# Row sums of |x - y|: the absolute values of the last row go to PSUM instead of SBUF

## The chip, the cores and the metric

The kernel runs on one core of a Trainium2 chip. The metric is the device time of an execution in microseconds (us), lower is better. Of every kernel some executions are timed and one is profiled. A run counts as slow when it is over 1.5% above the fastest of the same kernel, and as unknown when it is a single one; all the timed runs compared here were of the fast state, and the granted clock in their records was 1.0. Ratios are computed as the mean time of one kernel's fast runs over the mean of the other's in the same rounds, so they aren't quite the ratios of the medians that are quoted. "The span" is the time from the first to the last instruction of the profiled run; it is some 1.6 us shorter than the device time (82.8 beside 84.4 us).

Engines: VectorE (DVE in the profile) subtracts, ScalarE (ACT) takes absolute values and sums, the sync engine (SPq) issues transfers (DMA) from HBM, where x and y lie. ACTIVATE is the name of ScalarE's instruction in the profile. TensorE has no work. SBUF and PSUM are the memories in which the kernels allocate their tensors; the kernel before keeps its rows and sums in SBUF alone.

## The reference

```python
x, y = randn(1024, 4096), randn(1024, 4096)      # float32
np.sum(np.abs(x - y), axis=-1)                    # 1024 sums, float32
```

## The kernel before

Each of the 128 partitions holds 8 rows of 4096 columns. Rows 0 to 3 of x and y are loaded whole; the later y rows go into the buffers of the earlier ones, each after the subtraction that frees it. Rows 5 and 6 are worked in halves, and the last row in five pieces of 1728, 1024, 640, 384 and 320 columns, so that little work is left after the last byte has come (1.04 us, from 80.27 to 81.31 us of the span).

```python
def sub(tx, ty, waits):                       # VectorE: tx = tx - ty, in place
    for s, v in waits:
        put(lambda: nc.vector.wait_ge(s, v))
    put(lambda: nc.vector.tensor_sub(out=tx, in0=tx, in1=ty).then_inc(s_sub, 1))
    count[0] += 1

def absum(tx, to, sem):                       # ScalarE: |tx| in place, its sum into one column
    put(lambda: nc.scalar.wait_ge(s_sub, count[0]))
    put(lambda: nc.scalar.activation(tx, tx, ABS, accum_out=to).then_inc(sem, 1))
    count[1] += sem is s_act
# ... rows 0 to 6 ...
for i, w in enumerate(PIECES):                # the last row
    c = slice(o, o + w)
    tx, ty = xb[:, H - 1, c], yb[:, H - 1, c]
    # ... (i == 2: a small reduce of the sums of rows 5 and 6) ...
    if i < n_part:                            # the first four pieces
        sub(tx, ty, [(s_piece[i], 32)])
        absum(tx, last[:, i:i + 1], s_end)
    else:                                     # the last piece: VectorE alone
        put(lambda: nc.vector.wait_ge(s_piece[i], 32))
        put(lambda: nc.vector.tensor_sub(out=last[:, n_part:n_part + w], in0=tx, in1=ty).then_inc(s_end, 1))
        put(lambda: nc.vector.wait_ge(s_end, n_part + 2))
        put(lambda: nc.vector.reduce_sum(out=ro[:, K - 1:K], in_=last, axis=AX, apply_absolute_value=True).then_inc(s_end, 1))
    o += w
put(lambda: nc.sync.wait_ge(s_end, n_part + 3))
put(lambda: nc.sync.dma_start(out=orr, in_=ro).then_inc(s_out, 16))
```

The closing reduce runs over ScalarE's four sums and the last piece's 320 differences together, and so it needs two engines: VectorE's last subtraction and ScalarE's last sum. In the trace a second instruction, ACTIVATION_READ_ACCUMULATOR (below: the accumulator read) of 185 to 188 ns, follows each of the 13 ACTIVATEs; the semaphore update that VectorE waits for is recorded on it, and comes 8 ns after its end.

Of the kernel before, what the change touches and what calls it, by code (L numbers as in the profile page):

```python
# [6 lines left out]
F32 = mybir.dt.float32  # L7
ABS = mybir.ActivationFunctionType.Abs
AX = mybir.AxisListType.X

F32 = mybir.dt.float32
ABS = mybir.ActivationFunctionType.Abs
# [6 lines left out]
class Entry:  # L19
# [5 lines left out]
    def put(self, emit, before="UnconditionalBranch"):  # L25
        nc = self.nc
        hook = nc.inst_callbacks[-1]
        lower = nc._always_lower_symbolic_ap
        nc.remove_inst_callback(hook)
        nc._always_lower_symbolic_ap = False  # L30
        here = nc.cur_bb.bb.instructions
        n = len(here)
        try:
            emit()
        finally:
            nc._always_lower_symbolic_ap = lower
            nc.push_inst_callback(hook)
        here = nc.cur_bb.bb.instructions
        main = nc.main_func.blocks[0].instructions
        while len(here) > n:  # L40
            mine = here.pop(n)
            first = next(i for i, x in enumerate(main) if x.engine == mine.engine and x.opcode == before)
            main.insert(first, mine)
# [22 lines left out]
@with_exitstack  # L66
def kernel(ctx, tc, x, y, axis, out):
    nc = tc.nc
    P = nc.NUM_PARTITIONS
    R, C = x.shape  # L70
    K = R // P
    xr = x.rearrange("(p k) c -> p k c", p=P, k=K)
    yr = y.rearrange("(p k) c -> p k c", p=P, k=K)
    orr = out.rearrange("(p k) -> p k", p=P, k=K)
    assert sum(PIECES) == C and sum(HALVES) == C
    n_part = len(PIECES) - 1
    n2 = len(HALVES)
    H = K // 2
    entry = Entry(nc)
    put = entry.put  # L80


    def sbuf(name, shape):
        return nc.alloc_sbuf_tensor(name, shape, F32, align_bytes=256).ap()

    xa = sbuf("xa_rows", [P, H, C])
    xb = sbuf("xb_rows", [P, H, C])

    yb = sbuf("yb_rows", [P, H, C])
    ro = sbuf("ro_sums", [P, K])  # L90
    half = sbuf("half_sums", [P, 2, n2])

    last = sbuf("last_piece", [P, n_part + PIECES[-1]])

    s_first = tc.alloc_semaphore("s_first")
    s_xb = tc.alloc_semaphore("s_xb")
    s_row = [tc.alloc_semaphore(f"s_row{k}") for k in range(H - 1)]
    s_piece = [tc.alloc_semaphore(f"s_piece{i}") for i in range(len(PIECES))]
    s_sub = tc.alloc_semaphore("s_sub")
    s_act = tc.alloc_semaphore("s_act")  # L100
    s_end = tc.alloc_semaphore("s_end")

    s_out = nc.alloc_semaphore("s_out")


    for r in (slice(0, 1), slice(1, H)):
        put(lambda: nc.sync.dma_start(out=xa[:, r, :], in_=xr[:, r, :]).then_inc(s_first, 16), before="Drain")
    put(lambda: nc.scalar.dma_start(out=yb, in_=yr[:, 0:H, :]).then_inc(s_first, 16))
    put(lambda: nc.sync.dma_start(out=xb[:, 0:H - 1, :], in_=xr[:, H:K - 1, :]).then_inc(s_xb, 16))
    for k in range(H - 1):  # L110
        put(lambda: nc.sync.wait_ge(s_sub, k + 1))
        put(lambda: nc.sync.dma_start(out=yb[:, k, :], in_=yr[:, H + k, :]).then_inc(s_row[k], 16))
    o = 0
    for i, w in enumerate(PIECES):
        c = slice(o, o + w)
        put(lambda: nc.sync.dma_start(out=xb[:, H - 1, c], in_=xr[:, K - 1, c]).then_inc(s_piece[i], 16))  # L116
        if i == 0:
            put(lambda: nc.sync.wait_ge(s_sub, H))
        put(lambda: nc.sync.dma_start(out=yb[:, H - 1, c], in_=yr[:, K - 1, c]).then_inc(s_piece[i], 16))  # L119
        o += w  # L120


    count = [0, 0]

    def sub(tx, ty, waits):
        for s, v in waits:
            put(lambda: nc.vector.wait_ge(s, v))
        put(lambda: nc.vector.tensor_sub(out=tx, in0=tx, in1=ty).then_inc(s_sub, 1))  # L128
        count[0] += 1

    def absum(tx, to, sem):
        put(lambda: nc.scalar.wait_ge(s_sub, count[0]))
        put(lambda: nc.scalar.activation(tx, tx, ABS, accum_out=to).then_inc(sem, 1))  # L133
        count[1] += sem is s_act

    for k in range(H):
        sub(xa[:, k, :], yb[:, k, :], [(s_first, 48)] if k == 0 else [])
        absum(xa[:, k, :], ro[:, k:k + 1], s_act)
    sub(xb[:, 0, :], yb[:, 0, :], [(s_xb, 16), (s_row[0], 16)])
    absum(xb[:, 0, :], ro[:, H:H + 1], s_act)  # L140

    for k in (1, 2):
        o = 0
        for i, w in enumerate(HALVES):
            c = slice(o, o + w)
            sub(xb[:, k, c], yb[:, k, c], [(s_row[k], 16)] if i == 0 else [])
            absum(xb[:, k, c], half[:, k - 1, i:i + 1], s_act)
            o += w
    done56 = count[1]
    o = 0  # L150
    for i, w in enumerate(PIECES):
        c = slice(o, o + w)
        tx, ty = xb[:, H - 1, c], yb[:, H - 1, c]
        if i == 2:
            put(lambda: nc.vector.wait_ge(s_act, done56))
            put(lambda: nc.vector.reduce_sum(out=ro[:, K - 3:K - 1], in_=half, axis=AX).then_inc(s_end, 1))  # L156
        if i < n_part:
            sub(tx, ty, [(s_piece[i], 32)])
            absum(tx, last[:, i:i + 1], s_end)
        else:  # L160
            put(lambda: nc.vector.wait_ge(s_piece[i], 32))
            put(lambda: nc.vector.tensor_sub(out=last[:, n_part:n_part + w], in0=tx, in1=ty).then_inc(s_end, 1))  # L162
# [6 lines that stand above are left out]
    entry.at_end(lambda: nc.sync.wait_ge(s_out, 16).then_inc(s_out, -16))  # L169
# [35 lines left out]
```

## Time and profile before

| What | Before |
|---|---|
| Median of the first three runs | 84.38 us (84.36 to 84.47) |
| Span of the profiled run | 82.8 us |
| VectorE, ScalarE busy | 36.4 us (44%), 31.5 us (38%) |
| Read from HBM | 33.55 MB, 405 GB/s over the span |
| ACTIVATEs of the last row (1728, 1024, 640, 384) | 1627, 1040, 726, 513 ns |
| Accumulator read | 186 ns |
| Last subtraction (320), closing reduce | 492, 491 ns |

Neither compute engine is busy half of the time: they wait for data (VectorE for the first of y until 41.1 us), and DMA's busy share is 94 to 100% in the stretches from 20 to 76.6 us. The chain of waits and the timeline of the end are shown in the prediction. There, each row's start and duration are in us, and an entry in brackets tells how long the engine was idle before it and for whom.

### The profile page before, as it was taken

Reading aid. Unit: us, or ns where it says so; the run is one execution under the profiler, and the core shown is the slowest. Engines: PE = TensorE matmul, PEld = TensorE weight load, DVE = VectorE, ACT = ScalarE, POOL = GpSimd, SP = SyncE. Lnnn points to the kernel's source line nnn. Section 1 sums busy time; section 2 is a strip of 40 time slices with the busy share of each in tenths; the row PEclk is TensorE's granted clock in tenths of the full one; section 3 lists DMA queues with packets and bytes.
Section 4 is the critical chain, followed back from the end, with each engine's and each line's share of the span. In section 5 each row is a group of like instructions: output and inputs, shape, how many; then the busy total and the mean of one; then the engine's idle time right before and its main releaser. Section 6 shows DMA issues by size and latency. Waiting matters only on the chain.

```text
span 82.8 us, 104 instructions
## 1 busy us (share of the span) xinstructions
DVE 36.4 (44%) x16; ACT 31.5 (38%) x27; POOL 0.2 (0%) x4
## 2 busy tenths in 40 slices
DVE  0000000000000000000199999999279898999772
ACT  2400000000000000000000988979690599999990
POOL 0000000000000000000000000000000000000000
DMA  5992999989999999998888999859999999999950
GB/s 127 404 807 103 538 538 435 451 388 451 435 451 435 419 467 419 404 451 380 380 380 380 451 617 451 380 253 404 475 388 467 419 404 406 427 413 412 401 195 2
DMA packets 2592, 33.56 MB, mean 405 GB/s; under 512 B 416, under 2 KB 928, under 8 KB 1696
## 3 DMA queue, kind: packets, MB, share of 16 engines
q1 hardware_dynamic: 2448, 25.17, 72.3%
q10 hardware_dynamic: 144, 8.39, 23.4%
HBM read 33.55 MB, written 0.00 MB: 405 GB/s over the span
## 4 chain that ended last, share of the span: by engine, by line
DMA 63%; DVE 22%; SPq 10%; issue 1%
DMA yb_rows<-in_y_dram 63%; DVE xa_rows L128 21%; SPq L116 6%; SPq L119 4%; DVE last_piece L162 1%; DVE ro_sums L164 1%
## 5 line engine op out<-in xcount | busy, mean ns | idle before, releaser
L128 DVE TENSOR_TENSOR xa_rows<-xa_rows,yb_rows 128x4096 f32<-128x4096 f32 x4 | 17.4, 4420 | 41.1 <-DMA yb_rows<-in_y_dram 41.1
L133 ACT ACTIVATE xa_rows<-xa_rows 128x4096 f32<-128x4096 f32 x4 | 14.5, 3617 | 44.5 <-DVE xa_rows L128 44.5
L128 DVE TENSOR_TENSOR xb_rows<-xb_rows,yb_rows 128x2048 f32<-128x2048 f32 (+5 forms) x9 | 17.9, 2015 | 3.5 <-DMA yb_rows<-in_y_dram 3.5
L133 ACT ACTIVATE xb_rows<-xb_rows 128x2048 f32<-128x2048 f32 (+5 forms) x9 | 15.1, 1681 | 3.0 <-DVE xb_rows L128 2.9
L133 ACT ACT_TABLE_LOAD x1 | 1.3, 1283 | 1.7 <-PEq L186 1.7
L133 ACT ACTIVATION_READ_ACCUMULATOR xb_rows<-xb_rows 128x1 f32 x9 | 1.7, 186 | 0.0
L133 ACT ACTIVATION_READ_ACCUMULATOR xa_rows<-xa_rows 128x1 f32 x4 | 0.7, 186 | 0.0
L162 DVE TENSOR_TENSOR last_piece<-xb_rows,yb_rows 128x320 f32<-128x320 f32 x1 | 0.5, 492 | 0.3 <-DMA yb_rows<-in_y_dram 0.3
L164 DVE TENSOR_REDUCE ro_sums<-last_piece 128x1 f32<-128x324 f32 x1 | 0.5, 491 | 0.0
L156 DVE TENSOR_REDUCE ro_sums<-half_sums 128x2 f32<-128x4 f32 x1 | 0.1, 150 | 0.0
L186 POOL MEMSET const-bfloat16-1.0<- 128x1 bf16 x1 | 0.1, 101 | 0.0
L186 POOL MEMSET const-uint8-127<- 128x1 uint8 x1 | 0.1, 101 | 0.0
L186 POOL MEMSET const-float32-0.0<- 128x1 f32 x1 | 0.1, 98 | 0.2 <-issue 0.2
L186 POOL MEMSET const-float32-1.0<- 128x1 f32 x1 | 0.1, 98 | 0.0
## 6 DMA issues: line engine op xcount, KB each, us to landing
xa_rows<-in_x_dram SPq DMA_DIRECT2D x1, 6144.0 KB, 36.9
xb_rows<-in_x_dram SPq DMA_DIRECT2D x1, 6144.0 KB, 54.4
yb_rows<-in_y_dram SPq DMA_DIRECT2D x3, 2048.0 KB, 15.4
xa_rows<-in_x_dram SPq DMA_DIRECT2D x1, 2048.0 KB, 17.0
xb_rows<-in_x_dram SPq DMA_DIRECT2D x1, 864.0 KB, 17.7
yb_rows<-in_y_dram SPq DMA_DIRECT2D x1, 864.0 KB, 15.8
xb_rows<-in_x_dram SPq DMA_DIRECT2D x1, 512.0 KB, 16.6
yb_rows<-in_y_dram SPq DMA_DIRECT2D x1, 512.0 KB, 17.4
```

Of the source, the lines that this page charges most:

```text
L116: put(lambda: nc.sync.dma_start(out=xb[:, H - 1, c], in_=xr[:, K - 1, c]).then_inc(s_piece[i], 16))
L119: put(lambda: nc.sync.dma_start(out=yb[:, H - 1, c], in_=yr[:, K - 1, c]).then_inc(s_piece[i], 16))
L128: put(lambda: nc.vector.tensor_sub(out=tx, in0=tx, in1=ty).then_inc(s_sub, 1))
L133: put(lambda: nc.scalar.activation(tx, tx, ABS, accum_out=to).then_inc(sem, 1))
L156: put(lambda: nc.vector.reduce_sum(out=ro[:, K - 3:K - 1], in_=half, axis=AX).then_inc(s_end, 1))
L162: put(lambda: nc.vector.tensor_sub(out=last[:, n_part:n_part + w], in0=tx, in1=ty).then_inc(s_end, 1))
L164: put(lambda: nc.vector.reduce_sum(out=ro[:, K - 1:K], in_=last, axis=AX, apply_absolute_value=True).then_inc(s_end, 1))
L186: nc = _bacc.Bacc("TRN2", target_bir_lowering=False, num_devices=1)
```

## The change

ScalarE's in-place output of the last row's first four pieces is written to a PSUM tensor instead. Nobody reads these values. The intent is a shorter ACTIVATE near the end of the kernel.

```diff
+    absd = nc.alloc_psum_tensor("abs_piece", [P, C], F32).ap()
...
-    def absum(tx, to, sem):
+    def absum(tx, to, sem, out=None):
         put(lambda: nc.scalar.wait_ge(s_sub, count[0]))
-        put(lambda: nc.scalar.activation(tx, tx, ABS, accum_out=to).then_inc(sem, 1))
+        put(lambda: nc.scalar.activation(tx if out is None else out, tx, ABS, accum_out=to).then_inc(sem, 1))
...
-            absum(tx, last[:, i:i + 1], s_end)
+            absum(tx, last[:, i:i + 1], s_end, absd[:, c])
```

## The prediction

The sum came to 84.38 + 0.00 = 84.38 us. The savings were its terms for ScalarE: the earlier ones were held to become idle time, the last one to lie beside the last subtraction, so that they counted as 0.00 in it.

> **What bounds the kernel now.** I read four views: the chain that ended last, to see which work sets the end; the list of groups with the shapes kept apart, for the durations of the instructions concerned; the waits, for who was kept idle; and the timeline of the last six microseconds, where the change takes place. The chain on the page:
>
> ```profile
> ## 4 chain that ended last, share of the span: by engine, by line
> DMA 63%; DVE 22%; SPq 10%; issue 1%
> DMA yb_rows<-in_y_dram 63%; DVE xa_rows L128 21%; SPq L116 6%; SPq L119 4%; DVE last_piece L162 1%; DVE ro_sums L164 1%
> ```
>
> ScalarE (ACT) isn't in it at all. The kernel reads 33.55 MB and the page's DMA rate is a mean of 405 GB/s; from 20 us to 76.6 us the stretches that I summed run at 408 to 427 GB/s with DMA busy for 94 to 100%. VectorE (DVE, 44% busy) and ScalarE (38%) follow the transfers. The timeline of the end (columns: start, duration, engine, line, operation, out<-in, shapes, and in brackets how long the engine sat idle before and for whom):
>
> ```profile
> 76.67 1.63 ACT L133 ACTIVATE xb_rows<-xb_rows 128x1728 f32<-128x1728 f32 x1
> 76.88 1.23 DVE L128 TENSOR_TENSOR xb_rows<-xb_rows,yb_rows 128x1024 f32<-128x1024 f32 x1 [0.28 <-DMA yb_rows<-in_y_dram]
> ...
> 78.21 0.19 ACT L133 ACTIVATION_READ_ACCUMULATOR xb_rows<-xb_rows 128x1 f32 x1
> 78.30 1.04 ACT L133 ACTIVATE xb_rows<-xb_rows 128x1024 f32<-128x1024 f32 x1
> 78.47 0.82 DVE L128 TENSOR_TENSOR xb_rows<-xb_rows,yb_rows 128x640 f32<-128x640 f32 x1 [0.30 <-DMA yb_rows<-in_y_dram]
> 79.25 0.19 ACT L133 ACTIVATION_READ_ACCUMULATOR xb_rows<-xb_rows 128x1 f32 x1
> 79.34 0.73 ACT L133 ACTIVATE xb_rows<-xb_rows 128x640 f32<-128x640 f32 x1
> 79.46 0.56 DVE L128 TENSOR_TENSOR xb_rows<-xb_rows,yb_rows 128x384 f32<-128x384 f32 x1 [0.17 <-DMA yb_rows<-in_y_dram]
> 79.97 0.19 ACT L133 ACTIVATION_READ_ACCUMULATOR xb_rows<-xb_rows 128x1 f32 x1
> 80.06 0.51 ACT L133 ACTIVATE xb_rows<-xb_rows 128x384 f32<-128x384 f32 x1
> 80.29 0.49 DVE L162 TENSOR_TENSOR last_piece<-xb_rows,yb_rows 128x320 f32<-128x320 f32 x1 [0.28 <-DMA yb_rows<-in_y_dram]
> 80.48 0.19 ACT L133 ACTIVATION_READ_ACCUMULATOR xb_rows<-xb_rows 128x1 f32 x1
> 80.82 0.49 DVE L164 TENSOR_REDUCE ro_sums<-last_piece 128x1 f32<-128x324 f32 x1
> 81.34 0.35 SPq L168 DMA_DIRECT2D out_dram<-ro_sums  x1
> ```
>
> Two things are to be seen. First, each of VectorE's last four subtractions was kept waiting by a transfer of y (0.17 to 0.30 us), none by ScalarE. Second, the closing reduce at L164 needs both the last subtraction and ScalarE's last sum. The subtraction ends at 80.29 + 0.49 = 80.78, and the reduce starts 0.04 later. ScalarE's last accumulator read ends at 80.48 + 0.19 = 80.67. A hand-over from VectorE to ScalarE took about the same 0.04 (the 384 subtraction ends at 79.46 + 0.56 = 80.02, its ACTIVATE starts at 80.06), so ScalarE alone would have let the reduce start at about 80.71. ScalarE has 80.82 - 80.71 = 0.11 us of slack there. VectorE's own list of waits confirms that nothing of ScalarE's held it:
>
> ```profile
> DVE xb_rows L128 <- DMA yb_rows<-in_y_dram: 1.1, 4, 0.4
> DVE last_piece L162 <- DMA yb_rows<-in_y_dram: 0.3, 1, 0.3
> ```
>
> [...] the 384 ACTIVATE lasts 513 ns and the 4096 one 3617 ns, so (3617 - 513)/3712 = 0.836 ns an element, which leaves 513 - 384 x 0.836 = 192 ns fixed, and the accumulator read follows the 384 ACTIVATE's start by 0.42 us, that is 0.10 us more than its elements take. The trace of before has no PSUM access, so the other side is not shown. [...]
>
> **The change part by part.** The instruction lists of the two kernels have the same rows on every engine in the same order; only the main output of four ACTIVATEs (1728, 1024, 640 and 384 columns) is in another memory. Nothing is added: nobody reads the absolute values, only the sums, which still go to the same SBUF column. No semaphore count, DMA or wait changes. The nine other ACTIVATEs stay in place.
>
> [...] The 1728 ACTIVATE starts at 76.67 because of the one before it, which is unchanged. [...] the 640 subtraction ends at 78.47 + 0.82 = 79.29, so the start is 79.33 instead of 79.34. The 384 one likewise waits for its subtraction (80.02) and starts at 80.06, as before. So from the 640 piece on ScalarE is held by VectorE and the earlier savings become idle time. [...] On the path: 0.00 us. Even four ACTIVATEs that cost nothing would leave the reduce at 80.82.
>
> Against it on the path: no instruction, transfer or wait is longer. The sum is 84.38 + 0 = 84.38 us.
>
> **The rivals.** (1) ScalarE writes PSUM more slowly than SBUF[...]. Since ScalarE is just caught up at the 640 and 384 pieces, a cost of d for each of the four would add up: the end moves by about 4d - 0.11, as only 0.01 us of idle time stands in the way (79.33 against 79.34). So d = 0.1 us makes 84.38 + 0.29 = 84.67, within 2%. For 2% (1.69 us) d must be (1.69 + 0.11)/4 = 0.45 us, 88% on top of the 384 one's 513 ns. If PSUM halved the rate for an element, the 3776 columns would cost 3776 x 0.836 = 3.16 us more: 84.38 + 3.16 - 0.11 = 87.4 us. Nothing in the trace speaks for that[...]. I give it 1%.
>
> (2) Fewer SBUF writes speed up VectorE or the transfers. The trace speaks against it for VectorE: the first 128x4096 subtraction ran alone (ScalarE started at 45.60, after it) and the other three beside ScalarE's writes, and all four took 4418 to 4426 ns. The subtractions also wait for data, so only the last one's 0.49 us and the reduce's 0.49 us could count; a tenth of these would be 0.1 us: 84.28. For the transfers, only the last 3.7 us could gain; at a few per cent that is 0.1 us too.
>
> (3) ScalarE's earlier finish moves something that starts a transfer. It can't: the sync engine's only waits before the output are on VectorE's subtractions, and all loads of the last row are issued by 67.57 + 1.76 = 69.33 us, before the first changed ACTIVATE.
>
> **Range and chances.** The expected effect is zero, with at most some 0.1 us either way, so the range is mostly the spread between runs. The three runs of before span 84.36 to 84.47; another round or chip may shift the DMA's pace, which sets 63% of the chain, by some tenths of a per cent: 0.3% is 0.25 us. I take 84.2 to 84.6. Faster by 2% would need 1.7 us; the whole stretch from the last arrival (80.27) to the end of the reduce (81.31) is only 1.04 us, and no part of that is ScalarE's: 0.5%. Slower by 2% is rival 1: 1%. The rest, 98.5%, is within 2%.
>
> **What would show it.** In the profile after: the four ACTIVATEs write abs_piece with durations below 1627, 1040, 726 and 513 ns[...]; ScalarE shows a new idle time ahead of the 640 or 384 one, released by VectorE; VectorE's waits in the last row still name transfers alone; the reduce starts 0.04 us after the last subtraction ends; the chain has no ScalarE in it. The prediction is wrong if the reduce is released by ScalarE's last accumulator read (rival 1), if subtractions of equal shape last differently or the last y piece lands earlier in time against the same DMA start (rival 2), or if fast runs of the two kernels differ by over 0.3% in the same rounds.

## The result, and the profile after

The changed kernel took 84.39 us (median of 4 runs, 84.29 to 84.44), the kernel before in the same rounds 84.42 us (4 runs, 84.36 to 84.58): ratio 0.9993, 95% interval 0.9978 to 1.0008. The interval leaves no room for a gain of 0.25%.

The chain that ended last, on the page of the changed kernel (its lines are numbered two higher than before):

```profile
## 4 chain that ended last, share of the span: by engine, by line
DMA 63%; DVE 22%; SPq 11%; issue 1%
DMA yb_rows<-in_y_dram 63%; DVE xa_rows L130 21%; SPq L118 6%; SPq L121 4%; DVE last_piece L164 1%; DVE ro_sums L166 1%
```

It has the same members as before with nearly the same shares, and still no ScalarE. The timeline of the last six microseconds of the changed kernel:

```profile
76.60 1.59 ACT L135 ACTIVATE abs_piece<-xb_rows 128x1728 f32<-128x1728 f32 x1
...
78.13 0.19 ACT L135 ACTIVATION_READ_ACCUMULATOR abs_piece<-xb_rows 128x1 f32 x1
78.22 1.01 ACT L135 ACTIVATE abs_piece<-xb_rows 128x1024 f32<-128x1024 f32 x1
78.44 1.51 DVE L130 TENSOR_TENSOR xb_rows<-xb_rows,yb_rows 128x640 f32<-128x640 f32 x2 [0.34 <-DMA yb_rows<-in_y_dram]
79.17 0.19 ACT L135 ACTIVATION_READ_ACCUMULATOR abs_piece<-xb_rows 128x1 f32 x1
79.30 0.71 ACT L135 ACTIVATE abs_piece<-xb_rows 128x640 f32<-128x640 f32 x1
79.94 0.19 ACT L135 ACTIVATION_READ_ACCUMULATOR abs_piece<-xb_rows 128x1 f32 x1
80.04 0.47 ACT L135 ACTIVATE abs_piece<-xb_rows 128x384 f32<-128x384 f32 x1
80.26 0.49 DVE L164 TENSOR_TENSOR last_piece<-xb_rows,yb_rows 128x320 f32<-128x320 f32 x1 [0.32 <-DMA yb_rows<-in_y_dram]
80.45 0.19 ACT L135 ACTIVATION_READ_ACCUMULATOR abs_piece<-xb_rows 128x1 f32 x1
80.79 0.49 DVE L166 TENSOR_REDUCE ro_sums<-last_piece 128x1 f32<-128x324 f32 x1
```

(The row x2 holds the subtractions of 640 and 384 columns.) The last subtraction ends at 80.26 + 0.49 = 80.75 and the reduce starts 0.04 later, as before. ScalarE's last accumulator read ends at 80.45 + 0.19 = 80.64, again 0.11 us before the subtraction's end.

But the same rows hold a surprise. The ACTIVATEs are shorter: 1595, 1006, 707 and 473 ns in the list of groups, against 1627, 1040, 726 and 513. Yet the distance from an ACTIVATE's start to its accumulator read's start has not followed:

| Columns | Duration before, after (ns) | Start to accumulator read, before | after |
|---|---|---|---|
| 1728 | 1627, 1595 | 78.21 - 76.67 = 1.54 us | 78.13 - 76.60 = 1.53 us |
| 1024 | 1040, 1006 | 79.25 - 78.30 = 0.95 | 79.17 - 78.22 = 0.95 |
| 640 | 726, 707 | 79.97 - 79.34 = 0.63 | 79.94 - 79.30 = 0.64 |
| 384 | 513, 473 | 80.48 - 80.06 = 0.42 | 80.45 - 80.04 = 0.41 |

What became shorter is the tail of the record that overlaps the next instruction. So there are two candidate reasons for the unchanged time: ScalarE gained time with each instruction and it lay beside other work (the prediction), or ScalarE gained nothing in the first place.

### The profile page after: what moved, and what is told of

The parts are those of the page before. It is cut to its first block, busy times and chain, and to the rows that moved or that the text cites. A ratio compares the mean times of both kernels' runs of the same rounds, so it can differ in the third digit from the quotient of the medians.

```text
span 82.8 us, 104 instructions
## 1 busy us (share of the span) xinstructions
DVE 36.4 (44%) x16; ACT 31.6 (38%) x27; POOL 0.2 (0%) x4
## 4 chain that ended last, share of the span: by engine, by line
DMA 63%; DVE 22%; SPq 11%; issue 1%
DMA yb_rows<-in_y_dram 63%; DVE xa_rows L130 21%; SPq L118 6%; SPq L121 4%; DVE last_piece L164 1%; DVE ro_sums L166 1%
## 5 line engine op out<-in xcount | busy, mean ns | idle before, releaser
L135 ACT ACTIVATE xb_rows<-xb_rows 128x2048 f32<-128x2048 f32 (+1 forms) x5 | 11.2, 2244 | 3.0 <-DVE xb_rows L130 3.0
L135 ACT ACTIVATE abs_piece<-xb_rows 128x1728 f32<-128x1728 f32 (+3 forms) x4 | 3.8, 945 | 0.0
L135 ACT ACTIVATION_READ_ACCUMULATOR xb_rows<-xb_rows 128x1 f32 x5 | 0.9, 186 | 0.0
L135 ACT ACTIVATION_READ_ACCUMULATOR abs_piece<-xb_rows 128x1 f32 x4 | 0.7, 186 | 0.0
```

The costliest lines, as they stand in the source:

```text
L135: put(lambda: nc.scalar.activation(tx if out is None else out, tx, ABS, accum_out=to).then_inc(sem, 1))
```

## The experiments

The theory: the end is set by the last transfer, the last subtraction and the reduce; ScalarE's last sum comes some 0.1 us too early to matter. Rivals: the reduce does wait for ScalarE; the end never answers to ScalarE, however late; fewer SBUF writes speed up VectorE or the transfers. And within the theory, the open question of how much a PSUM destination is worth to ScalarE.

### The changed kernel again, in five rounds

No edit.

> The changed kernel once more, in five rounds, so that a gain of a few tenths of a per cent would show. Theory (ScalarE's end lies beside the last subtraction): ratio to the kernel before 1.000 within 0.002, median 84.3 to 84.5 us. Rival (the closing reduce waited for ScalarE, so its earlier end counts): about 0.03 us less, which the time alone could hardly show; then the reduce would start within 0.05 us of ScalarE's last accumulator read, and not 0.04 us after the last subtraction. Rival (fewer SBUF writes speed up VectorE or the transfers): 0.1 us less or more, with shorter subtractions.

Measured: 84.37 us (5 runs, 84.31 to 84.46) against 84.36 us for the kernel before (9 runs); ratio 1.0004, interval 0.9990 to 1.0018. In its timeline the reduce starts at 80.78, 0.03 us after the last subtraction's end (80.26 + 0.49 = 80.75), while ScalarE had finished at 80.44 + 0.19 = 80.63. A gain of 0.2% is excluded.

### Next to no work in the last row's ACTIVATEs

```diff
-            absum(tx, last[:, i:i + 1], s_end, absd[:, c])
+            absum(tx[:, 0:8], last[:, i:i + 1], s_end, absd[:, o:o + 8])
```

> The four ACTIVATEs of the last row take 8 columns each (the last row's sums are wrong on purpose). This is the ceiling of anything that can be saved on them: 3744 of 3776 columns less, 3.1 us of ScalarE's busy time. Theory: the same time as the kernel before within 0.15 us (84.3 to 84.5), the reduce still starts 0.04 us after the last subtraction, at about 80.8 us of the span. Rival (ScalarE's end sets the reduce): 376 x 0.836 ns = 0.31 us less, about 84.07 us. Rival (ScalarE's accesses slow VectorE or the transfers): the subtractions of 1024, 640, 384 and 320 columns get shorter than 1225, 826, 557 and 493 ns.

Measured: 84.39 us (5 runs, 84.31 to 84.53), ratio 1.0006, interval 0.9994 to 1.0019. The result is wrong, as intended. From its timeline:

```profile
80.06 0.18 ACT L135 ACTIVATE abs_piece<-xb_rows 128x8 f32<-128x8 f32 x1 [0.43 <-DVE xb_rows L130]
80.17 0.19 ACT L135 ACTIVATION_READ_ACCUMULATOR abs_piece<-xb_rows 128x1 f32 x1
80.30 0.49 DVE L164 TENSOR_TENSOR last_piece<-xb_rows,yb_rows 128x320 f32<-128x320 f32 x1 [0.27 <-DMA yb_rows<-in_y_dram]
80.82 0.49 DVE L166 TENSOR_REDUCE ro_sums<-last_piece 128x1 f32<-128x324 f32 x1
```

ScalarE is done at 80.17 + 0.19 = 80.36 instead of 80.67, and the reduce starts at 80.82, the very time of the kernel before. Between 76 and 83 us ScalarE is busy for 1.85 us in place of 4.63 in the changed kernel, 2.8 us less where 3.1 were expected. The subtractions of 1024, 640, 384 and 320 columns take 1226, 824, 559 and 491 ns; before they took 1226, 824, 559 and 492. The last subtraction, which waits for the last transfer of y, starts at 80.30 us, against 80.29 in the kernel before. So no saving on these ACTIVATEs could shorten this kernel, and taking their accesses away gave VectorE and the transfers nothing.

### ScalarE made late by 1024 columns

```diff
+            if i == n_part - 1:
+                more = nc.alloc_sbuf_tensor("more_abs", [P, 1024], F32).ap()
+                put(lambda: nc.scalar.wait_ge(s_sub, count[0]))
+                put(lambda: nc.scalar.activation(more, xb[:, H - 1, 0:1024], ABS))
             absum(tx, last[:, i:i + 1], s_end, absd[:, c])
```

> One more ACTIVATE of 1024 columns (its result unused) on ScalarE ahead of that of the 384 columns. It should hold ScalarE for 1024 x 0.836 + 100 = 956 ns. Theory (0.11 us of slack, then ScalarE is on the path): 0.956 - 0.11 = about 0.85 us later, 85.2 us (85.05 to 85.4), the reduce released by ScalarE. Rival (the end doesn't answer to ScalarE at all): 84.4 us. Rival (no slack before): 0.96 us later, 85.35 us.

Measured: 85.21 us (4 runs: 85.12, 85.14, 85.28 and one of 86.02), against 84.36; the difference of the medians is 0.85 us. The ratio of the means, 1.0124 (1.0086 to 1.0163), is pulled up by the run of 86.02, which nothing on record explains. From its list of waits:

```profile
DVE ro_sums L170 <- ACT abs_piece L135: 0.9, 1, 0.9
```

And from its timeline, the added ACTIVATE, the last subtraction, the last rows of ScalarE and the reduce:

```profile
79.97 1.04 ACT L164 ACTIVATE more_abs<-xb_rows 128x1024 f32<-128x1024 f32 x1
80.19 0.49 DVE L168 TENSOR_TENSOR last_piece<-xb_rows,yb_rows 128x320 f32<-128x320 f32 x1 [0.27 <-DMA yb_rows<-in_y_dram]
80.92 0.48 ACT L135 ACTIVATE abs_piece<-xb_rows 128x384 f32<-128x384 f32 x1
81.34 0.19 ACT L135 ACTIVATION_READ_ACCUMULATOR abs_piece<-xb_rows 128x1 f32 x1
81.55 0.49 DVE L170 TENSOR_REDUCE ro_sums<-last_piece 128x1 f32<-128x324 f32 x1 [0.87 <-ACT abs_piece L135]
```

The delay is 80.92 - 79.97 = 0.95 us, and the end moved by 0.85. The difference is the slack. The hand-over from ScalarE to the reduce is also seen here: 81.34 + 0.19 = 81.53 to 81.55, 0.02 us; it is 0.03 us in the traces of the four later runs in which ScalarE releases the reduce.

### ScalarE made late by 256 columns

The same edit with 256 in both places.

> The added ACTIVATE of late_scalar_1024 with 256 columns: 256 x 0.836 + 100 = 314 ns of ScalarE's time. Theory (a slack of 0.11 to 0.13 us, then the end answers one for one): 0.314 - 0.12 = about 0.2 us later than before (84.5 to 84.65), ratio about 1.0023; with 0.85 us for the 1024 one, the line through the two has a slope of 1 and meets zero at 0.1 us of delay. Rival (the end answers in proportion, no slack): 0.31 us later.

Measured: 84.59 us (5 runs, 84.53 to 84.67) against 84.41 us (11 runs), 0.18 us later; ratio 1.0023, interval 1.0011 to 1.0036. In its timeline the added ACTIVATE starts at 80.15 and the next at 80.45, a delay of 0.30 us, and the reduce was idle 0.22 us for ScalarE. The line through the two points has the slope (0.85 - 0.18)/(0.95 - 0.30) = 1.03 and meets zero at 0.30 - 0.18/1.03 = 0.13 us. That is the slack of ScalarE by the kernels' times, with the delays read from the traces. It is loose: the interval of this run alone (0.11 to 0.36% of 84.41, or 0.09 to 0.30 us later) would allow a slack between none and 0.2 us. The two traces are tighter. The last subtraction ends at 80.19 + 0.49 = 80.68 in the one and at 80.37 + 0.49 = 80.86 in the other; 0.04 later, at 80.72 and 80.90, the reduce could have started, and it started at 81.55 and 81.08. Delays of 0.95 and 0.30 us moved it by 0.83 and 0.18 us, so the slack is 0.12 us in both.

### What a PSUM destination and a PSUM source are worth to ScalarE

ScalarE waits for the first data until 45 us. In that time it runs six trains of six ACTIVATEs of 384 columns, each train waiting for the one before. Two readings were set against each other: that a PSUM destination shortens the step, as the prediction had it, and that the source alone decides the step.

```diff
+    put(lambda: nc.vector.memset(src_s, 1.0).then_inc(s_src, 1))      # in SBUF
+    put(lambda: nc.vector.memset(src_p, 1.0).then_inc(s_src, 1))      # in PSUM
+    put(lambda: nc.scalar.wait_ge(s_src, 2))
+    for acc in (False, True):
+        for src, psum in ((src_s, False), (src_s, True), (src_p, False), (src_p, True)):
+            # ... with acc: only the two trains that read src_s ...
+            for t in range(6):
+                # ... dst: a fresh place in dst_sb or in PSUM; more: accum_out with acc ...
+                put(lambda: nc.scalar.activation(dst, src, ABS, **more).then_inc(s_src, 1))
+            put(lambda: nc.scalar.wait_ge(s_src, 2 + 6 * trains))
```

> In the time in which ScalarE waits for the first data anyway, trains of six ACTIVATEs of 384 columns: SBUF to SBUF, SBUF to PSUM, PSUM to SBUF, PSUM to PSUM, then SBUF to SBUF and SBUF to PSUM with a sum. The time of the kernel should not change (84.3 to 84.6 us). [...] Other reading, from the trace after (the accumulator reads follow their ACTIVATEs' starts by 1.53, 0.95, 0.64 and 0.41 us with PSUM and 1.54, 0.95, 0.63 and 0.42 without): the step from start to start depends on the source alone, equal within 5 ns for the two destinations, and only the recorded duration is shorter by 20 to 40 ns with PSUM[...].

Measured: 84.64 us, a single run, 0.04 us outside what was expected; from one run of an unknown state nothing is concluded on the time. The first four trains in its timeline (each row is a whole train: start, and the time from the first start to the last end):

```profile
2.96 2.59 ACT L156 ACTIVATE dst_sb<-src_sb 128x384 f32<-128x384 f32 x6
5.57 2.55 ACT L156 ACTIVATE abs_piece<-src_sb 128x384 f32<-128x384 f32 x6
8.15 2.40 ACT L156 ACTIVATE dst_sb<-abs_piece 128x384 f32<-128x384 f32 x6
10.59 2.39 ACT L156 ACTIVATE abs_piece<-abs_piece 128x384 f32<-128x384 f32 x6
```

A train's length is five steps from start to start and the last one's duration. With the mean durations of the list of groups (508 ns for SBUF to SBUF and 476 for SBUF to PSUM, both over the plain and summing trains together; 506 for PSUM to SBUF; 492 for PSUM to PSUM):

| Source, destination | Step from start to start |
|---|---|
| SBUF, SBUF | (2.59 - 0.508)/5 = 0.416 us |
| SBUF, PSUM | (2.55 - 0.476)/5 = 0.415 us |
| PSUM, SBUF | (2.40 - 0.506)/5 = 0.379 us |
| PSUM, PSUM | (2.39 - 0.492)/5 = 0.380 us |

Over whole trains the destination is worth about 1 ns a step and the source 36 ns. The first step of each train is longer than the others, however, and not by the same amount. Read from the second start to the last, with narrow windows on the same trace, the steps are (5.04 - 3.39)/4 = 0.412 and (7.65 - 6.00)/4 = 0.412 us with the source in SBUF, and (10.03 - 8.54)/4 = 0.372 and (12.46 - 10.98)/4 = 0.370 us with the source in PSUM. So in the steady part no gain from the destination can be read, and the source, which the change left in SBUF, is worth some 41 ns. It is one trace, with 384 columns. The two trains with sums, as in the kernel, agree on the destination; these are the first and the last start of each:

```profile
13.02 0.52 ACT L156 ACTIVATE dst_sb<-src_sb 128x384 f32<-128x384 f32 x1
...
15.56 0.51 ACT L156 ACTIVATE dst_sb<-src_sb 128x384 f32<-128x384 f32 x1
...
16.19 0.49 ACT L156 ACTIVATE abs_piece<-src_sb 128x384 f32<-128x384 f32 x1
...
18.73 0.47 ACT L156 ACTIVATE abs_piece<-src_sb 128x384 f32<-128x384 f32 x1
```

(15.56 - 13.02)/5 and (18.73 - 16.19)/5 are both 0.508 us. So the PSUM destination took 19 to 40 ns off the recorded durations of the kernel's four ACTIVATEs, and no more than the 0.01 us that can be read off the time until ScalarE's next instruction started. With a sum, the next instruction is the accumulator read, and the reduce started 0.02 to 0.03 us after that one's end wherever ScalarE released it, so the waiting engine didn't see the saving. Without a sum it can be seen: the second train waits for the end of the first and the third for that of the second, and the starts lie 5.57 - 2.96 = 2.61 us apart with the destination in SBUF and 8.15 - 5.57 = 2.58 us with that in PSUM (with the source in PSUM 2.44 and 2.43). No experiment was made on that case.

### The change where ScalarE does set the end

Three kernels with the last two pieces moved from 384 and 320 to 448 and 256 columns, which makes ScalarE the later one: the kernel before with that edit (last_256_sbuf), the changed kernel with it (last_256_psum), and the latter with the 448 differences written to PSUM as well, to a place of their own (last_256_source).

```diff
-PIECES = [1728, 1024, 640, 384, 320]
+PIECES = [1728, 1024, 640, 448, 256]
```

and for last_256_source:

```diff
+            bank7 = absd[:, 3584:3584 + w] if i == n_part - 1 else None
-            sub(tx, ty, [(s_piece[i], 32)])
+            sub(tx, ty, [(s_piece[i], 32)], bank7)          # the subtraction's output
+            if i == n_part - 1:
+                absum(bank7, last[:, i:i + 1], s_end)        # in place in PSUM
+            # ... else: as in the changed kernel; sub() takes the output as a new argument ...
```

> The kernel before (absolute values in SBUF) with the last two pieces of 448 and 256 columns in place of 384 and 320, which puts ScalarE in the lead of the end. Estimate from the durations: the subtraction of 448 columns takes 0.63 us and ends at about 80.25, ScalarE's ACTIVATE starts at 80.28, its accumulator read runs from 80.75 to 80.94; the last subtraction ends at 80.71; so the reduce (0.42 us) starts at about 80.96, released by ScalarE, and ends at 81.38 in place of 81.31. Time 0 to 0.15 us above the kernel before.

> The same with the absolute values in PSUM: the change in a setting in which ScalarE's end does set the reduce. [...] Reading from the trains (the step depends on the source alone): 0.47 us after the start in both, no gain even here. In the times both are within 0.1 us of last_256_sbuf.

> last_256_psum with the difference of the 448 columns written to PSUM by VectorE, so that ScalarE reads from PSUM too. From the trains (0.379 us a step with a source in PSUM, 0.416 in SBUF): the accumulator read comes 0.43 us after its ACTIVATE's start in place of 0.47. If the subtraction of 448 columns isn't longer with its output in PSUM, the reduce comes 0.04 us earlier than in last_256_psum; if VectorE pays more for PSUM, this is lost again. Times within 0.1 us of last_256_psum; the profile has to tell.

Measured, beside 84.41 us for the kernel before: 84.48 us for SBUF (ratio 1.0011, interval 0.9999 to 1.0023), 84.42 us for PSUM (1.0009, 0.9996 to 1.0022), 84.48 us for the PSUM source (1.0020, 1.0005 to 1.0035; two of its six runs were at 84.70 and 84.76). The intervals overlap, so the times don't tell the three apart. The timelines do. Last_256_sbuf:

```profile
80.26 0.58 ACT L133 ACTIVATE xb_rows<-xb_rows 128x448 f32<-128x448 f32 x1
...
80.74 0.19 ACT L133 ACTIVATION_READ_ACCUMULATOR xb_rows<-xb_rows 128x1 f32 x1
80.96 0.42 DVE L164 TENSOR_REDUCE ro_sums<-last_piece 128x1 f32<-128x260 f32 x1 [0.27 <-ACT xb_rows L133]
```

Last_256_psum:

```profile
80.37 0.55 ACT L135 ACTIVATE abs_piece<-xb_rows 128x448 f32<-128x448 f32 x1
...
80.85 0.19 ACT L135 ACTIVATION_READ_ACCUMULATOR abs_piece<-xb_rows 128x1 f32 x1
81.07 0.42 DVE L166 TENSOR_REDUCE ro_sums<-last_piece 128x1 f32<-128x260 f32 x1 [0.23 <-ACT abs_piece L135]
```

Last_256_source:

```profile
80.25 0.53 ACT L135 ACTIVATE abs_piece<-abs_piece 128x448 f32<-128x448 f32 x1
...
80.69 0.19 ACT L135 ACTIVATION_READ_ACCUMULATOR abs_piece<-abs_piece 128x1 f32 x1
80.91 0.42 DVE L170 TENSOR_REDUCE ro_sums<-last_piece 128x1 f32<-128x260 f32 x1 [0.18 <-ACT abs_piece L135]
```

In all three the reduce is released by ScalarE. From the ACTIVATE's start to its accumulator read it is 80.74 - 80.26 = 0.48 us with SBUF, 80.85 - 80.37 = 0.48 with the PSUM destination, 80.69 - 80.25 = 0.44 with the PSUM source. From the ACTIVATE's start to the reduce's start it is 0.70, 0.70 and 0.66 us. So even where ScalarE's end counts, the change gives nothing within 0.01 us, and reading from PSUM gives 0.04; this rests on one trace of each, since the times resolve neither. The subtraction that wrote to PSUM took 632 ns against 626 and 625, so it gave almost nothing of that back. No version beats the original: the pieces of 384 and 320 already leave the two engines within about 0.12 us of each other.

Not tried: all thirteen ACTIVATEs into PSUM. They write 32448 columns a partition (32768 less the last 320) and the tensor has 4096, so they would have to overwrite each other. How ScalarE's longer stretches would fare is left open; the trains speak against a gain.

## Why the prediction was right

- **The bound.** It said that the last transfer of y, the last subtraction and the reduce set the end. Shown: the chain is unchanged, and with next to no ScalarE work the reduce starts at the same 80.82.
- **The slack of 0.11 us.** It was read from 80.71 against 80.82. Two delays put it at 0.12 us in their traces, and loosely at 0.13 us by the kernels' times. The small difference fits the hand-over, taken as 0.04 us from VectorE to ScalarE, and seen as 0.02 to 0.03 us from ScalarE to the reduce (80.82 - 80.67 - 0.03 = 0.12).
- **The saving on ScalarE: wrong in substance.** The estimate took time off from each start to the next. This did not happen: the step is 0.416 against 0.415 us in the trains, and 0.42 against 0.41 in the kernel for the 384 piece. The estimate went by the destination, where the trains show the source to decide the step, with some 41 ns. Because this saving was worth zero on the path anyway, the sum was not touched. The prediction's tale of how the saving turns into idle time ahead of the 640 piece is therefore void: ScalarE had no such saving to lose. The sign that it named did appear, by luck: from the start of the 1024 piece's accumulator read to the 640 ACTIVATE it is 79.30 - 79.17 = 0.13 us, and was 79.34 - 79.25 = 0.09. But ScalarE had begun the row 0.07 us earlier in that trace (76.60 against 76.67) and the 640 subtraction only 0.03 us earlier (78.44 against 78.47).
- **Durations.** It expected each to be shorter; measured were 32, 34, 19 and 40 ns less. The direction was right; the size that it gave is cut with the estimate behind it.
- **Rival 1, slower PSUM writes.** Not seen: no ACTIVATE became longer, that of 1728 columns (1595 against 1627 ns) included.
- **Rival 2, fewer SBUF writes.** Tested directly with the ACTIVATEs of 8 columns, and rejected: the subtractions kept their durations within 1 ns. The last transfer of y took 12.69 us from issue to landing in the changed kernel, against 12.70 before.
- **Rival 3, an earlier transfer.** The transfers are issued before 70 us in the changed kernel too, and the chain into the last subtraction is again a transfer of y (63%).
- **Time and range.** 84.38 us was predicted and 84.39 measured; the spread between runs (84.29 to 84.44) was indeed all that there was.

## What to carry to other kernels

Before shortening an engine's work near the end, read which of the two engines releases the closing instruction, and how early the other one is; here it was 0.12 us early, and no saving on it could show. A shorter duration in the profile isn't yet a faster engine: compare the distances from start to start, since the tail of an instruction's record can overlap the next one (here an ACTIVATE recorded with 1.63 us had its successor start 1.54 us after its own start). Where an ACTIVATE with a sum does set the end, look at where its input lies, not at where an unused output goes: the input was worth 0.04 us here, in the trace.
